# When the FFN output weights' sums are begun, and which queue carries their copies: a fused decoder layer on Trainium2

## The chip, the cores and the metric

The kernel runs on one core of one Trainium2 chip. The metric is device time in microseconds (us) of one execution, inputs in the device's memory at its start and the output written at its end. The engines of the core are called as in the profile: PE (TensorE, matmuls; PEld its weight loads), DVE (VectorE), ACT (ScalarE), POOL (GpSimd), SP (SyncE). SPq, ACTq and POOLq stand for the instruction streams in which these engines issue DMAs. Each engine works through its stream in order.

## The reference

One layer of a decoder trunk on a sequence of 512 tokens of width 1024, in fp32:

```python
h = rms_norm(x, norm_mix)
q_a, k_a, v_a, u_b, gate_b, gate_c, g_a, g_b = split(h @ w_in)        # 1024 -> 5120
o_a = stick_breaking_attention(q_a, k_a, v_a)                         # 8 heads of 64, causal
y_b = gate_b * causal_depthwise_conv(gate_c * u_b, conv_w)            # 3 taps, 512 channels
merged = sigmoid(g_a) * (o_a @ w_branch_a) + sigmoid(g_b) * (y_b @ w_branch_b)
x = x + merged @ w_mix_out
x = x + memory_cross_attention(rms_norm(x, norm_mem_q), rms_norm(mem, norm_mem_kv),
                               w_mem_q, w_mem_kv, w_mem_o)            # 4 heads of 256, 256 memory tokens
gate, up = split(rms_norm(x, norm_ffn) @ w_ffn_in)                    # 1024 -> 2 x 2816
x = x + (silu(gate) * up) @ w_ffn_out                                 # 2816 -> 1024
return rms_norm(x, norm_final)
```

## The kernel before, in words

Activations lie with channels on the 128 partitions and the 512 tokens along the free axis, so that a width of 1024 is eight tiles. An fp32 product is made of three matmuls in a shorter format: each operand is split into a high part (a cast on ACT) and a low part (a subtraction on DVE), and high by high, high by low and low by high are added up (`mm3`, L161 to L163). `load_w` brings a weight tile of 512 KB (tile `wr`, L148, issued on SP), casts it to `wh` (L156, ACT) and subtracts for `wl` (L157, DVE); four buffers of each are in turn. So a late cast or split makes a `wr` buffer free late, and the load that is to use it is issued late.

The stages, with their places in the profiled execution: the input projection and the attention (to about 160 us), the merge with its gates and branch projections (a loop over eight output tiles m), the mixer's output projection (`residual` on `w_mix_out`, eight tiles; tile `r`; to about 344), the memory's keys (`km`, eight tiles, 344 to 367), half of the values (`vm`), the query forms and the rest of the values (367 to 400), the four memory heads (scores `sc`, maximum `mx`, bound `nb`, exps `pr`, transposes `pt`, output `om`; to about 464), the memory's output projection (`residual` again, on `w_mem_o`), the FFN's first weights (`ws`, `wg`, `a`), and the FFN's output weights in the last stage.

Some products use sums of weight quarters, in the manner of Strassen's method. Two kinds of sums are made ahead of their use.

- The sums of the FFN's output weights, 11 sets j = 0 to 10 (`out_sums`). A set is two copies from DRAM to DRAM (768 and 256 KB, L569, on SP) and then three adds by POOL's DMAs (512, 256 and 256 KB, L572), which add to the tile in DRAM where it lies (`sums`). A step waits for the landing of the step before. The last stage reads them, from about 700 us on.
- The sums of the memory's query weights, one per head: a load of 1 MB (`pq`, L642), three additions on DVE, a store of 1 MB to DRAM (`qsums`, L652), in the merge and the mixer's output projection.

What sets the order of the sums is a counter of ticks. `job(at, steps, lag)` puts the steps of a set at ticks `at`, `at + lag` and so on; `tick(last)` issues what stands at the present tick behind the instruction `last` in program order. The steps of the sums do not wait for that instruction on the chip, only for their data and for their place in their engine's stream. Ticks come 17 times in the attention (0 to 16), 8 times in the merge (17 to 24), at every second tile of the mixer's output projection (25 to 28), twice in the keys' loop (29, 30), once after the first values (31), and once per memory head (32 to 35). `SUMS_AT` is the list of the first ticks, and `SPARSE` says how many sets take two ticks per step in place of one.

Between the mixer's output projection and the memory heads, the factor r1 of the second norm is needed with tokens on partitions. It goes through DRAM (`turned_row`): a row `vrow` of 2 KB is stored (L226, `row`) and loaded back as `vr` (L228), both on SP; ACT then makes `ry` of it (L125, L126) and DVE `ra` and `r` (L129 to L133). The same helper, on POOL's stream, serves a later norm (`r0b`, `row`, `rt`).

`pair_forms` (L810 to L812) loads the query weights and their sums and splits them into `wf`; `q_product` (L834 to L855) multiplies them (`qz`, `qv`) and copies the results out (`qs`, `qb`).

Of the kernel before, what the change touches and what calls it, by code (L numbers as in the profile page):

```python
# [34 lines left out]
FIRST = 4  # L35
LIGHT = 3
BEHIND = 6
SUMS_AT = (0, 2, 4, 20, 22, 24, 25, 26, 27, 28, 30)
SPARSE = 3

O_Q, O_K, O_V, O_U, O_GB, O_GC, O_A, O_B = 0, 512, 1024, 1536, 2048, 2560, 3072, 4096

# [2 lines left out]
def hybrid_layer(ctx: ExitStack, tc: tile.TileContext, xT_d, memT_d, mem_d, cols_d, wv_d, win_d,  # L45
                 wbr_d, wmix_d, wmq_d, wmk_d, wmv_d, wmo_d, wfi_d, wfo_d, gfin_d, out):
    nc = tc.nc
# [16 lines left out]
    def nm(s):  # L64
        count[0] += 1
        return f"{s}{count[0]}"

    def unit(s, cols=512):
        return upool.tile([P, cols], F32R, tag="u", name=nm(s), padded_shape=[P, 512])

    def tmp(s, cols=512):
        return tpool.tile([P, cols], F32, tag="t", name=nm(s), padded_shape=[P, 512])

    def f(ap):
        return ap.bitcast(F32)

    def mmtile(s, pool=None, tag="mm"):
        return (pool or pmm).tile([P, 512], F32, tag=tag, name=nm(s))
# [28 lines left out]
    def after(i, earlier):  # L107
        for e in earlier:
            tc.add_manual_dep(i.ins, e.ins.name, mybir.DependencyInfo(
                mybir.DependencyClass.NoSync, mybir.DependencyReason.DATA), reason="order")  # L110
# [33 lines left out]
    def load_w(src, cols=P):  # L144

        k = D // cols
        raw = wpool.tile([P, D], F32, tag="wr", name=nm("wr"))
        i = nc.sync.dma_start(raw, src)  # L148
        loads.append(i)
        if count[1] < FIRST:  # L150
            count[1] += 1
            chained(i)
        hi = wpool.tile([P, k, cols], F32R, tag="wh", name=nm("wh"))
        lo = wpool.tile([P, k, cols], F32R, tag="wl", name=nm("wl"))
        h2, l2 = (t.rearrange("p k c -> p (k c)") for t in (hi, lo))
        after(nc.scalar.copy(h2, raw), lead[-1:])  # L156
        lows.append(nc.vector.tensor_tensor(out=l2, in0=raw, in1=f(h2), op=ALU.subtract))  # L157
        return hi, lo
# [8 lines left out]
    def gemm(ps, w, act, k0=0):  # L167

        n = len(act)
        for k in range(n):  # L170
            if k == n // 2 and midway:
                midway.pop()()
            mm3(ps, (w[0][:, k0 + k, :], w[1][:, k0 + k, :]), act[k], k == 0, k == n - 1)
# [277 lines left out]
    def scores(p, kt):  # L451
        c0, n = span(kt)
        keys = slice(kt * P, (kt + 1) * P)
        zs[p, kt] = []
        for hs in heads_of(kt):
            bank = ztile("z")
            zs[p, kt].append(bank)
            for i, h in enumerate(hs):
                for part in range(2):
                    nc.tensor.matmul(bank[:, i * n:(i + 1) * n], ks[p][h][:, keys],  # L460
                                     qs[p][h][part][:, c0:], start=i + part == 0, stop=part == 1,
                                     skip_group_check=True)
        for hs, bank in zip(heads_of(kt), zs[p, kt]):
            w = len(hs) * n
            z = bank[:, :w]
            e = tmp("e")[:, :w]
            nc.scalar.activation(e, z, AF.Abs)
            nc.scalar.activation(e, e, AF.Exp, scale=-1.0)
            nc.scalar.activation(e, e, AF.Ln, bias=1.0)
            nc.vector.scalar_tensor_tensor(out=e, in0=z, scalar=0.0, in1=e, op0=ALU.max,  # L470
                                           op1=ALU.add)
            causal(by_head(e, n))
            urgent.append(lambda *last, e=e, hs=hs: fails(p, kt, hs, e, n, last))
# [86 lines left out]
    def quarters(w):  # L560
        return w.rearrange("p (s c) -> p s c", s=4)

    def in_dram(tag):
        return dpool.tile([P, 4, 512], F32, tag=tag, name=nm(tag))

    sums = [in_dram(f"sums{j}") for j in range(NJ)]

    def copied(to, of):
        return lambda *last: after(nc.sync.dma_start(to, of), last)  # L569

    def added(to, of):
        return lambda *last: after(nc.gpsimd.dma_start(to, of, accum_op=ALU.add), last)  # L572

    def out_sums(j):
        t, w = sums[j], quarters(wfo_d[j])
        return ([copied(t[:, 1:4, :], w[:, 1:4, :]), copied(t[:, 0:1, :], w[:, 3:4, :])],
                [added(t[:, 0:4:3, :], w[:, 0:2, :])], [added(t[:, 1:2, :], t[:, 0:1, :])],
                [added(t[:, 2:3, :], t[:, 1:2, :])])

# [2 lines left out]
    def job(at, steps, lag=1):  # L582
        for n, some in enumerate(steps):
            jobs.setdefault(at + n * lag, []).extend(some)

    def tick(*last):
        for some in jobs.pop(started[0], ()):
            some(*last)
        started[0] += 1
# [14 lines left out]
    settle_behind()  # L604
    qsums = [in_dram(f"qsums{h}") for h in range(MH)]
    for j, n in enumerate(SUMS_AT):
        job(n, out_sums(j), 2 if j < SPARSE else 1)

    for i in range(len(steps) + 1):
        tick(*exps[-1:])  # L610
# [10 lines left out]
        if i + 1 < len(steps):  # L621
            to = lambda: scores(*steps[i + 1])
# [15 lines left out]
    mg, mgs, qraws = [], [], {}  # L638

    def form_load(h, last):  # L640
        qraws[h] = prepool.tile([P, 4, 512], F32, tag="pq", name=nm("pq"))
        after(nc.sync.dma_start(qraws[h], quarters(wmq_d[h])), last)  # L642

    def form_sums(h, last, *steps):

# [3 lines left out]
                                          op=ALU.add), last)  # L649

    def form_store(h):
        nc.sync.dma_start(qsums[h], qraws.pop(h))  # L652

    def mem_split(k2, last):
        mk = xpool.tile([P, 2, MEM], F32, tag="x", name=nm("mk"))
# [15 lines left out]
    for m in range(KD):  # L671
        sig = []
        for j in range(2):
            if (m, j) not in gates:
                gate(m, j)
            t = gates.pop((m, j))
# [5 lines left out]
        w = load_w(wbr_d[m])  # L682
# [74 lines left out]
    def residual(w_dram, act, old, gain, formed):  # L757


        xs, xf = [], []  # L760
        acc = tmp("acc")
        for m in range(KD):
            w = load_w(w_dram[m])
            ps = mmtile("r")
            gemm(ps, w, act)
            if old is None:
                xm = xpool.tile([P, S], F32, tag="x", name=nm("x"))
                after(nc.sync.dma_start(xm, xT_d[m * P:(m + 1) * P, :]), sigmoids[m // 2 - 4])
            else:
                xm = old[m]  # L770
            nc.vector.tensor_tensor(out=xm, in0=ps, in1=xm, op=ALU.add)
            xs.append(xm)
            if old is None and m % 2:
                tick(lows[-1])
                if qraws:
                    form_store(MH - 1)
            raw = f(unit("xr"))
            nc.scalar.activation(raw, xm, AF.Copy, scale=gain[:, m:m + 1])
            if m % 2:
                xf.append(formed(even, raw))  # L780
            else:
                even = raw
            if m == 0:
                nc.scalar.activation(acc, xm, AF.Square)
            else:
                sq = tmp("sq")
                nc.scalar.activation(sq, xm, AF.Square)
                nc.vector.tensor_tensor(out=acc, in0=acc, in1=sq, op=ALU.add)
        return xs, xf, (lambda: squares_mean(acc, TT))

    x1, x1f, mean1 = residual(wmix_d, merged, None, g_q, flat_forms)
    mean1 = mean1()
    stick.close()
# [82 lines left out]
    for m in range(KD):  # L876
        w = load_w(wmk_d[m])
# [8 lines left out]
        t = tmp("km", MEM)  # L886
# [52 lines left out]
    for h in range(MH):  # L939
        q = qgot[h]  # L940
        scs = []
        for t2 in range(2):
            ps = ztile("sc")
            scs.append(ps)
            for i in range(2):
                t = 2 * t2 + i
# [5 lines left out]
        for t2 in range(2):  # L952
# [14 lines left out]
            for i in range(2):  # L967
                t = 2 * t2 + i
# [25 lines left out]
        for j in range(2):  # L994
# [3 lines left out]
            for m in range(MT):  # L998
                w = vm[m][c // 512]
                mm3(ps, (w[0][:, sl], w[1][:, sl]), ptr[m], m == 0, m == MT - 1)  # L1000
            om.append(split(ps, "om"))

    lead.append(qacts[-3])
    x2T, x2f, mean2 = residual(wmo_d, om, x1, g_ffn, forms_of)


# [141 lines left out]
    m = NF - 1  # L1148
# [96 lines left out]
    def one_cast(j):  # L1245
        if j % 2 == 0:
            n = min(2, NJ - j)
            raw = ows["q3"] = wpool.tile([P, 2, 512], F32, tag="wr", name=nm("wr"))
            nc.sync.dma_start(raw[:, :n, :], wfo_d[j:j + n, :, 0:512].rearrange("j p c -> p j c"))
        raw = ows["q3"][:, j % 2, :]  # L1250
        pool, tag = (fpool, "wg") if j in (BEHIND, BEHIND + 2) else (wpool, ("wh", "wl")[j % 2])
        w = pool.tile([P, 2, 512], F32R, tag=tag, name=nm("wq"))
        nc.scalar.copy(w[:, 0, :], raw)
        ows[5, j] = w[:, 0, :], w[:, 1, :]
        return raw, *ows[5, j]
# [75 lines left out]
    n = uses.index((NF - 2, 5))  # L1331
# [23 lines left out]
    with tc.manual_schedule(engines={mybir.EngineType.PE, mybir.EngineType.Activation,  # L1355
# [58 lines left out]
        for j in range(2, NJ - 2):  # L1414
# [6 lines left out]
            if NJ - 2 - LIGHT <= j + 1 < NJ - 2 + 1:  # L1421
                n = j + 1 - (NJ - 2 - LIGHT)
                if n < LIGHT:
                    t34_of(n, halves(acts[n][1])[0])
        last = NJ - 2, NJ - 1
# [93 lines left out]
        w = one_cast(NJ - 1)  # L1519
# [184 lines left out]
```

## Time and profile before

| | |
|---|---|
| time, median of 3 runs | 835.94 us (835.62 to 836.13) |
| profiled execution, its own time | 837.15 us |
| its span, first to last instruction | 835.4 us |
| mean granted TensorE clock | 0.998 |
| PE busy | 826.5 us (99% of the span) |
| ACT busy | 481.8 us (58%) |
| issues of the sums: copies on SP, adds on POOL | 22, 33 |
| DMA bytes by SP's queues and by POOL's | 130.96 MB, 23.21 MB |

Rows of the profile give the engine, the line, the operation, the tile written and the tiles read; in the views by time the first number is the start in us from the span's start, the second the length, and a bracket at the end tells how long the engine had been idle before and what ended that. "DMA share" is the mean busy share of the 16 DMA engines. A DMA's "us to landing" counts from its issue.

### The profile page before, as it was taken

The page shows a single profiled execution, that of the slowest core. Times are in us where ns is not written, and L with a number is a line of the kernel's source. Part 1 is how long each engine was busy: PE and PEld are TensorE (multiplying, and loading weights), DVE is VectorE, ACT ScalarE, POOL GpSimd, SP SyncE. Part 2 cuts the span into 40 slices and gives each one's busy share as a digit, 9 for nine tenths or more (in the row PEclk, how much of TensorE's full clock was granted, in tenths as well). Part 3 has the DMA queues.
Part 4 walks back from the last instruction along what each step waited for, and adds up shares of the span by engine and source line. Part 5 has one row for each costly group of instructions (what it writes and reads, how often), then busy time and mean ns, then how long its engine had stood idle before and what let it go on. Part 6 is the DMA issues. An engine that isn't in the chain of part 4 may idle for free.

```text
span 835.4 us, 12382 instructions
## 1 busy us (share of the span) xinstructions
PE 826.5 (99%) x4518; PEld 718.7 (86%) x4518; DVE 689.6 (83%) x1146; ACT 481.8 (58%) x836; POOL 105.9 (13%) x131
## 2 busy tenths in 40 slices
PE   9999999999999999999999999999999999999996
PEld 7888888888888888888999789999999999888885
DVE  7879899995665557865677689999999999999886
ACT  7567777674332345645665556645555555576664
POOL 0022331120010011210000131111111110000301
PEclk9999999999999999999999999999999999999999
DMA  8667965224588999898445626677777773565552
GB/s 303 202 189 179 222 141 121 82 81 171 216 225 291 253 312 294 194 218 279 125 136 189 167 50 170 165 179 189 207 179 196 181 181 97 166 217 198 178 187 100
DMA packets 58926, 155.24 MB, mean 186 GB/s; under 512 B 6545, under 2 KB 7825, under 8 KB 57842
## 3 DMA queue, kind: packets, MB, share of 16 engines
q1 hardware_dynamic: 46226, 130.96, 46.6%
q0 software_dynamic: 12352, 23.21, 18.5%
q8 instruction: 35, 0.57, 0.3%
q10 hardware_dynamic: 288, 0.28, 0.1%
q14 instruction: 25, 0.20, 0.1%
HBM read 144.08 MB, written 29.37 MB: 208 GB/s over the span
## 4 chain that ended last, share of the span: by engine, by line
PE 95%; DMA 2%; DVE 1%; ACT 1%; issue 0%; DVEq 0%; SPq 0%; ACTq 0%
PE z L1078 13%; PE p L1389 12%; PE pr L161 8%; PE pr L162 8%; PE pr L163 8%; PE y L1073 5%; PE r L161 3%; PE r L163 3%; PE r L162 3%; PE v L288 3%; PE y L1081 2%; PE v L1073 2%; PE qz L834 2%; PE br L162 2%; PE br L161 2%; PE br L163 2%
## 5 line engine op out<-in xcount | busy, mean ns | idle before, releaser
L156 ACT CAST wh<-wr 128x1024 fp32r<-128x1024 f32 x76 | 79.7, 1051 | 113.0 <-issue 45.1
L161 PE MATMUL pr<-xgh,wh 128*128 128x512 f32 x288 | 112.7, 391 | 0.0
L162 PE MATMUL pr<-xgl,wh 128*128 128x512 f32 x288 | 112.4, 390 | 0.0
L163 PE MATMUL pr<-xgh,wl 128*128 128x512 f32 x288 | 112.3, 390 | 0.0
L157 DVE TENSOR_TENSOR wl<-wr,wh 128x1024 fp32r<-128x1024 f32 x76 | 93.6, 1232 | 9.8 <-ACT wh L156 9.5
L163 PEld LDWEIGHTS pr<-xgh,wl 128*128 128x128 f32 x288 | 54.1, 188 | 11.5
L161 PEld LDWEIGHTS pr<-xgh,wh 128*128 128x128 f32 x288 | 54.1, 188 | 10.6
L162 PEld LDWEIGHTS pr<-xgl,wh 128*128 128x128 f32 x288 | 54.1, 188 | 10.5
L1026 POOL DMA_DIRECT2D ws<-in_w_ffn_in_dram x22 | 26.6, 1207 | 237.5 <-PE pt L987 57.1
L1078 PE MATMUL z<-xd,wf 128*128 128x256 f32 x360 | 47.5, 282 | 0.0
L1110 ACT COPY sa<-z 128x256 f32<-128x256 f32 x44 | 16.5, 374 | 52.1 <-PE z L1078 52.0
L1078 PEld LDWEIGHTS z<-xd,wf 128*128 128x128 f32 x360 | 44.9, 190 | 0.1
L1170 DVE TENSOR_TENSOR wf<-wg,wf 128x1024 fp32r<-128x1024 f32 (+1 forms) x44 | 43.1, 979 | 1.5
L1170 DVE TENSOR_TENSOR wl<-wr,wh 128x1024 fp32r<-128x1024 f32 x33 | 41.1, 1247 | 3.6 <-ACT wh L1237 3.6
L368 DVE TENSOR_TENSOR g<-pr,r0b 128x512 f32<-128x512 f32 x16 | 11.0, 689 | 34.2 <-PE pr L163 34.2
L1237 ACT CAST wh<-wr 128x1024 fp32r<-128x1024 f32 x33 | 34.5, 1049 | 6.9 <-PE xt L1474 2.5
L1078 PE MATMUL z<-xf,wf 128*128 128x256 f32 x264 | 35.4, 283 | 0.0
L1078 PE MATMUL z<-xc,wf 128*128 128x256 f32 x264 | 35.1, 282 | 0.0
L1078 PEld LDWEIGHTS z<-xf,wf 128*128 128x128 f32 x264 | 33.4, 192 | 0.1
L1078 PEld LDWEIGHTS z<-xc,wf 128*128 128x128 f32 x264 | 33.0, 190 | 0.0
L572 POOL DMA_DIRECT2D sums<-sums x22 | 18.5, 851 | 94.7 <-DMA sums<-in_w_ffn_out_dram 47.4
L572 POOL DMA_DIRECT2D sums<-in_w_ffn_out_dram x11 | 15.7, 1469 | 98.7 <-DMA sums<-in_w_ffn_out_dram 98.2
(377 smaller groups left out, 2313.8 us busy)
## 6 DMA issues: line engine op xcount, KB each, us to landing
wr<-in_w_in_dram SPq DMA_DIRECT2D x36, 512.0 KB, 4.1
ws<-in_w_ffn_in_dram SPq DMA_DIRECT2D x22, 512.0 KB, 4.6
wg<-in_w_ffn_in_dram SPq DMA_DIRECT2D x22, 512.0 KB, 4.5
ws<-in_w_ffn_in_dram POOLq DMA_DIRECT2D x22, 512.0 KB, 5.8
wr<-sums SPq DMA_DIRECT2D x22, 512.0 KB, 4.4
sums<-in_w_ffn_out_dram SPq DMA_DIRECT2D x11, 768.0 KB, 8.1
wr<-in_w_ffn_out_dram SPq DMA_DIRECT2D x16, 512.0 KB, 4.5
sums<-in_w_ffn_out_dram POOLq DMA_DIRECT2D x11, 512.0 KB, 10.2
```

The lines of the kernel that those rows point to most:

```text
L156: after(nc.scalar.copy(h2, raw), lead[-1:])
L157: lows.append(nc.vector.tensor_tensor(out=l2, in0=raw, in1=f(h2), op=ALU.subtract))
L161: nc.tensor.matmul(ps, a[0], b[0], start=start, stop=False, **kw)
L162: nc.tensor.matmul(ps, a[0], b[1], start=False, stop=False, **kw)
L163: nc.tensor.matmul(ps, a[1], b[0], start=False, stop=stop, **kw)
L572: return lambda *last: after(nc.gpsimd.dma_start(to, of, accum_op=ALU.add), last)
L1026: nc.gpsimd.dma_start(s13, a[:, 0:4:3, :], accum_op=ALU.add)
L1073: nc.tensor.matmul(ps, hi, both[0], start=i < 3 and k == 0, stop=False, skip_group_check=True)
L1078: nc.tensor.matmul(ps[:, :HS], a, b, start=i < 3 and k == 0 and j == 0, stop=k == KP - 1 and j == 2, skip_group_check=True)
L1170: nc.vector.tensor_tensor(out=lo, in0=src, in1=f(hi), op=ALU.subtract)
L1237: nc.scalar.copy(hi, raw)
L1389: nc.tensor.matmul(res[i][s2], a[:, ts], b, start=j == 0 and n == 0, stop=n == 2 and j == (BEHIND - 1 if (i, s2) == (5, 1) else NJ - 1))
```

## The change

The list of first ticks is new: sets 0 to 3 are in the attention, three ticks apart, and the last three begin at ticks 32, 34 and 36. `SPARSE` is 4. The copies of sets 4 to 10 are issued on ACT; so are the loads and stores of the query weights' sums. `residual` now ticks in the memory's output projection too (ticks 36 to 39). Line numbers after L577 are higher by one in the changed kernel.

```diff
-SUMS_AT = (0, 2, 4, 20, 22, 24, 25, 26, 27, 28, 30)
-SPARSE = 3
+SUMS_AT = (0, 3, 6, 9, 19, 22, 26, 30, 32, 34, 36)
+SPARSE = 4
...
-    def copied(to, of):
-        return lambda *last: after(nc.sync.dma_start(to, of), last)
+    def copied(queue, to, of):
+        return lambda *last: after(queue.dma_start(to, of), last)
...
-    def out_sums(j):
+    def out_sums(j, queue):
         t, w = sums[j], quarters(wfo_d[j])
-        return ([copied(t[:, 1:4, :], w[:, 1:4, :]), copied(t[:, 0:1, :], w[:, 3:4, :])],
+        return ([copied(queue, t[:, 1:4, :], w[:, 1:4, :]),
+                 copied(queue, t[:, 0:1, :], w[:, 3:4, :])],
                 [added(t[:, 0:4:3, :], w[:, 0:2, :])], [added(t[:, 1:2, :], t[:, 0:1, :])],
...
-        job(n, out_sums(j), 2 if j < SPARSE else 1)
+        job(n, out_sums(j, nc.sync if j < SPARSE else nc.scalar), 2 if j < SPARSE else 1)
...
-        after(nc.sync.dma_start(qraws[h], quarters(wmq_d[h])), last)
+        after(nc.scalar.dma_start(qraws[h], quarters(wmq_d[h])), last)
...
-        nc.sync.dma_start(qsums[h], qraws.pop(h))
+        nc.scalar.dma_start(qsums[h], qraws.pop(h))
...
-            if old is None and m % 2:
+            if m % 2:
                 tick(lows[-1])
```

In the rows of the order below, the number behind a name tells one buffer of it from another; `sums_374` to `sums_384` are the sets 0 to 10, in both kernels.

SP's stream before, where the loads for the memory's keys begin: the copies of sets 8 and 9 stand between them.

```order
L148 DMA wr_3347<-in_w_mem_k_dram 128x1024
L569 DMA sums_382<-in_w_ffn_out_dram 128x1536
L569 DMA sums_382<-in_w_ffn_out_dram 128x512
L148 DMA wr_3378<-in_w_mem_k_dram 128x1024
L148 DMA wr_3425<-in_w_mem_k_dram 128x1024
L569 DMA sums_383<-in_w_ffn_out_dram 128x1536
L569 DMA sums_383<-in_w_ffn_out_dram 128x512
L148 DMA wr_3456<-in_w_mem_k_dram 128x1024
```

After the change the loads there stand alone:

```order
L148 DMA wr_3268<-in_w_mix_out_dram 128x1024
L148 DMA wr_3337<-in_w_mem_k_dram 128x1024
L148 DMA wr_3368<-in_w_mem_k_dram 128x1024
L148 DMA wr_3415<-in_w_mem_k_dram 128x1024
L148 DMA wr_3446<-in_w_mem_k_dram 128x1024
```

The copies of sets 8 and 9 have left this place, and no copy of a set stands in SP's stream behind the attention any more.

ACT's stream before, at the end of the keys' loop, where the query forms begin:

```order
L156 CAST wh_3670<-wr_3668 128x1024
L887 COPY km_3602<-km_3585 128x256
L894 CAST kmh_3575<-km_3602 128x256
L811 CAST wf_3697<-wr_3696 128x1024
L811 CAST wf_3703<-wr_3702 128x1024
```

And after:

```order
L156 CAST wh_3656<-wr_3654 128x1024
L888 COPY km_3590<-km_3573 128x256
L569 DMA sums_381<-in_w_ffn_out_dram 128x1536
L895 CAST kmh_3563<-km_3590 128x256
L569 DMA sums_381<-in_w_ffn_out_dram 128x512
L812 CAST wf_3682<-wr_3681 128x1024
L812 CAST wf_3688<-wr_3687 128x1024
```

The two copies of set 7 stand there now; before, set 10's copies were issued from SP's stream at that tick.

DVE's stream before, in the last memory head, between the last weight split ahead of the scores and the exps' bounds:

```order
L157 TENSOR_TENSOR wl_4778<-wr_4775,wh_4777 128x1024
L955 TENSOR_REDUCE mx_4576<-sc_4550 128x2
L955 TENSOR_REDUCE mx_4588<-sc_4563 128x2
L958 SCALAR_TENSOR_TENSOR nb_4578<-mx_4576,r1s 128x2
L958 SCALAR_TENSOR_TENSOR nb_4590<-mx_4588,r1s 128x2
```

And after:

```order
L956 TENSOR_REDUCE mx_4567<-sc_4541 128x2
L157 TENSOR_TENSOR wl_4774<-wr_4771,wh_4773 128x1024
L959 SCALAR_TENSOR_TENSOR nb_4569<-mx_4567,r1s 128x2
L956 TENSOR_REDUCE mx_4579<-sc_4554 128x2
L959 SCALAR_TENSOR_TENSOR nb_4581<-mx_4579,r1s 128x2
```

The split of the fourth weight of the memory's output projection has moved from ahead of the first maximum to behind it. On PE, seven matmuls of that projection (`r`) stand ahead of the first scores of this head, where one stood; the eighth stands among the scores, where three stood.

## The prediction

> **What bounds the kernel now.** I read the page first, for who is busy.
>
> ```profile
> span 835.4 us, 12382 instructions
> PE 826.5 (99%) x4518; PEld 718.7 (86%) x4518; DVE 689.6 (83%) x1146; ACT 481.8 (58%) x836; POOL 105.9 (13%) x131
> ```
>
> TensorE (PE) is busy for 826.5 of 835.4 us. A change that touches no matmul can win only PE's 8.9 us of idle time and whatever is hidden inside "busy". So the second view is PE's own waits, and the third its busy time by stretches of the span. The columns of that one are length, PE, weight load, DVE, ACT and POOL busy time, the granted clock, the DMA engines' share and GB/s.
>
> ```profile
> PE warm L248 <- DVE neg L92: 1.4, 1, 1.4
> PE qz L834 <- ACT qs L845: 0.7, 1, 0.7
> PE vm L161 <- DVE km L888: 0.4, 1, 0.4
> ...
> 354.00:366.00 12.00, 12.00 (x69) 10.51 (x68) 5.87 (x11) 4.61 (x11) 1.66 (x2) 1.00 1.05 240
> 374.00:386.00 12.00, 11.29 (x74) 10.17 (x73) 8.20 (x11) 6.72 (x10) 1.17 (x1) 1.00 0.94 296
> 440.00:460.00 20.00, 20.00 (x137) 17.93 (x135) 13.69 (x28) 11.27 (x25) 0.79 (x1) 1.00 0.61 206
> 518.00:528.00 10.00, 10.00 (x75) 9.48 (x74) 9.83 (x19) 6.39 (x9) 1.69 (x4) 1.00 0.66 164
> 820.00:836.00 16.00, 9.01 (x54) 7.83 (x52) 9.57 (x26) 7.99 (x22) 2.70 (x2) 0.89 0.35 131
> ```
>
> The last stretch leaves 7.0 us that this change does not touch, and the first wait, 1.4 us at the start, is as far from it. What remains are two waits in the middle: vm and qz, both in 366 to 386. A third fence, of PE's rows in order of time, shows how much they really cost.
>
> ```profile
> 366.96 0.39 PE L161 MATMUL vm<-wh,mg 128*128 128x512 f32 x1
> 368.52 0.50 PE L161 MATMUL vm<-wh,mg 128*128 128x512 f32 x1 [0.42 <-DVE km L888]
> 369.08 0.39 PE L163 MATMUL vm<-wh,mg 128*128 128x512 f32 x1
> 378.63 0.39 PE L163 MATMUL vm<-wh,mg 128*128 128x512 f32 x1
> 384.59 0.28 PE L834 MATMUL qv<-xfh,wf 128*128 128x256 f32 x1
> 385.58 0.39 PE L834 MATMUL qz<-xfh,wf 128*128 128x256 f32 x1 [0.71 <-ACT qs L845]
> ```
>
> From 369.08 to 378.63 there are 42 steps of 512 columns, 0.227 us each, with no wait. From 366.96 to 369.08 there are five, which at that pace take 1.14 us and here take 2.12: stall 1 costs 0.98. A 256-column step takes about half of that, 0.12; the one from 384.59 to 385.58 takes 0.99: stall 2 costs 0.87. Together 1.85 us is what is to be had, just above the 1.67 us (0.2% of 835.94) that a measurement of this kernel can tell from no change.
>
> The chain of waits names what both hang on, and ScalarE's and GpSimd's rows show it standing.
>
> ```profile
> 354.73 5.07 DMA row<-vrow
> 359.81 5.61 DMA vr<-row
> 366.10 1.22 DVE wl L157
> ...
> 374.86 7.54 DMA wr<-in_w_mem_q_dram
> ...
> 365.45 0.30 ACT L125 ACTIVATE ry<-vr,eps_t 128x4 f32<-128x4 f32 x1 [4.30 <-DMA vr<-row]
> 384.21 1.05 ACT L156 CAST wh<-wr 128x1024 fp32r<-128x1024 f32 x1 [1.11 <-DVE qa L843]
> ...
> 356.10 0.85 POOL L572 DMA_DIRECT2D sums<-sums  x1 [3.56 <-DMA sums<-sums]
> 362.56 0.81 POOL L572 DMA_DIRECT2D sums<-sums  x1 [5.61 <-DMA sums<-in_w_ffn_out_dram]
> ```
>
> The factor r1 of the second norm goes through DRAM: 2 KB out, 2 KB back, 10.7 us, in a stretch where the DMA share is 1.05 and adds of the sums are on their way (two wait for one another's landings on POOL here). ACT works in order and stands 4.30 us on it; DVE stands behind ACT, and behind DVE the split (wl) of the first memory value weights, which vm needs: stall 1. The same lateness passes through the weight slots that such splits free to the query load of 374.86, its cast, and the weight cast of 384.21 that stands ahead of the copy qs: stall 2.
>
> **The change part by part.** *Times of the sums.* Of the eleven sets, j=3 to 10 had their copies at ticks 20 to 30; now j=3 is in the attention, j=4, 5, 6 are at 19, 22, 26, j=7 at 30 and j=8 to 10 at 32, 34, 36. The order puts the first copy of j=6 right behind the weight cast that now runs at 306.12 (last row below). From there the copies, the big add and the two small ones take 8.1 + 10.2 + 6.7 + 6.7 us, to 339 (an estimate). The copies of j=7 stand behind km's last copy to SBUF, near 368, as PE leaves km at 366.96. Between them no set is on the way, and the round trip meets only weight loads. Its price is bounded above by its own 10.7 us and below by the same pair of hops in 518 to 528, where the share is 0.66:
>
> ```profile
> sums<-in_w_ffn_out_dram SPq DMA_DIRECT2D x11, 768.0 KB, 8.1
> sums<-in_w_ffn_out_dram POOLq DMA_DIRECT2D x11, 512.0 KB, 10.2
> sums<-sums POOLq DMA_DIRECT2D x22, 256.0 KB, 6.7
> ...
> row<-r0b POOLq DMA_DIRECT2D x1, 2.0 KB, 4.5
> rt<-row POOLq DMA_DIRECT2D x1, 2.0 KB, 2.9
> ...
> 306.12 1.05 ACT L156 CAST wh<-wr 128x1024 fp32r<-128x1024 f32 x1 [3.18 <-PE r L162]
> ```
>
> That is 7.4 us. I take it, since weight loads alone are what ran there too: r1's row lands at 362.1 in place of 365.4, 3.3 us earlier. Stall 1 needs 1.0 us of that, and the copy qs must come 1.9 us earlier, because PE is there 1.0 us sooner. Both fit, with 1.4 us to spare: minus 1.85 us. At the other end of the bound nothing is won. By the Trainium skill ("DMA: Bandwidth & Descriptors", the part on the anatomy of one DMA), a DMA has about 2.0 us of fixed cost, which would make two hops 4.0 us and the gain no larger, since the stalls are gone before; the rows with 2.9 and 4.5 us say that it is more here.
>
> *Copies and query sums on ScalarE's queue.* 14 copies, four loads (pq) and four stores (qsums), 22 issues in all, leave SP's stream and enter ACT's.
>
> ```profile
> 373.13 1.14 SPq L569 DMA_DIRECT2D sums<-in_w_ffn_out_dram  x2
> ...
> 0.79 0.40 ACTq L236 DMA_DIRECT2D gcol<-in_columns_dram  x1
> ...
> 437.25 0.56 ACT L969 ACTIVATE pr<-sc,nb,r1s 128x256 f32<-128x256 f32 x1 [1.61 <-DVE nb L958]
> ```
>
> An issue costs 0.40 us on ACT's one row and 0.57 on SP's pairs: 8.8 to 12.5 us of an engine that is busy 58%. The residual lets ACT idle for 3.18 us ahead of a cast (306.12), which a pair of 0.8 to 1.14 fits into; a store that waits for DVE's sum holds only casts that wait for PE anyway. In the heads the two copies of a set stand before and after pr, where 1.61 us are free. I cost it at nothing; if that cover went, each copy would put 0.40 to 0.57 us on pr and on the transposes behind it. On SP the loads behind 373.13 are issued 1.14 us sooner, which adds to the slack of stall 2. The sum has nothing in it for faster landings. By the Trainium skill (same page, "Issuing engines are not separate DMA queues") transfers of all issuing engines run on the same 16 DMA engines, so that this move saves issue time only; no run here shows it, since the load of 7.54 us right behind two copies may be late by the engines' load or by its queue's order.
>
> *Fourth set in the attention.* PE has no idle time there. The additions cost POOL 0.85 us each beside its mask selects, and the sets start three ticks apart in place of two. Bounds: 0, and 0.85 if one select on the path stands behind one add. I take 0, because PE's waits name nothing in the attention now.
>
> *Late sets, head 3.* The order moves matmuls of the output projection (r) ahead of the last scores, and a weight split between mx and nb.
>
> ```profile
> 455.57 0.56 ACT L969 ACTIVATE pr<-sc,nb,r1s 128x256 f32<-128x256 f32 x1 [3.85 <-DVE nb L958]
> 457.69 0.60 PE L987 MATMUL pt<-ident,pr 128*128 128x128 f32 x4
> ```
>
> Before, pr starts at 455.57 and PE comes to pt at 457.69, without a wait. Now four more r steps of 0.23 us stand ahead of the scores' end and one fewer behind it: PE comes to pt 0.7 us later. The split of 1.22 us (the wl row) between mx and nb, less the half of the scores that is no longer waited for, makes pr late by about 0.7 too (estimates from these rows). Between 0 and 0.7 us are at stake; I take 0, because the two move together.
>
> *Late sets, FFN's start.* POOL's loads of the FFN weights now have adds between them; such a load may come late:
>
> ```profile
> 471.90 1.21 POOL L1026 DMA_DIRECT2D ws<-in_w_ffn_in_dram  x1 [11.45 <-DVE c L713]
> 490.19 0.62 ACT L1059 CAST wf<-ws 128x512 fp32r<-128x512 f32 x1 [2.65 <-PE r L162]
> ```
>
> From its issue to its use there are 18.3 us. If it stood behind an add that lands in 10.2, 8 us would be left for it. Nothing.
>
> Sum: minus 0.98 and minus 0.87, the rest 0: minus 1.85. Against the profiled execution's own 837.15 us (the span and 1.75 around it) this gives 835.30; the median of the runs is 1.21 below the profiled execution, so 834.1.
>
> **The rivals.** *A, half of it.* The two stalls are not equally safe. The copies of j=7 still fall beside the query loads, as those of j=10 did, and now on a queue of their own. If the load of 374.86 keeps its landing at 382.4, stall 2 stays and grows by the 1.0 us that PE is early: a gain between 0 and 0.98, 834.9 to 835.9. For it speaks the 0.94 share in 374 to 386; against it the 3.3 us.
>
> *B, no change.* The 1.05 share of 354 to 366 may come from the weight loads themselves, which now run sooner: the round trip keeps its 10.7 us, 835.9. Against it: the software queue of the adds is what goes.
>
> *C, slower: a late weight in head 3.* By the order, two sets are now copied between 436 and 460, beside the exps (pr) of heads 2 and 3, where the share is 0.61 and mem_o's weights come in.
>
> ```profile
> wr<-in_w_mem_o_dram SPq DMA_DIRECT2D x8, 512.0 KB, 3.8
> DMA to landing us min/median/max: 6.0/8.1/15.5
> ...
> 440.56 0.69 DVE L812 TENSOR_TENSOR wf<-wr,wf 128x512 fp32r<-128x512 f32 x1
> ```
>
> The second row is that of the copies. The fourth mem_o weight is issued at about 441.3, when the query split of 440.56 has freed its slot, and its cast (1.05) and split (1.22) now stand ahead of pr and nb. With 3.8 us it is there at 445; with the copies' median at 449.4, still early. For pr at 455.57 as now, cast and split must start by 453.3 (455.57 less 1.05 and 1.22): from a landing of 12.0 us on, PE waits one for one. At the copies' largest, 15.5, it is 3.5 us, and the time 834.1 + 3.5 = 837.6. The gain is eaten at 13.9 us. By the Trainium skill (same page, on queues, rings and completion order) each DMA engine takes turns between queues with work, packet by packet; a load on SP's queue would then share its engines with ACT's copies rather than go ahead of them, about twice 3.8 us, which this place bears.
>
> **How the numbers follow.** Forecast 0.48 (833.6 to 834.6), A 0.23, B 0.14, C or the attention's 0.85 with the stalls kept 0.15. The forecast falls below 834.27 (faster by over 0.2%) in some three quarters of its cases: 0.37. The last case, counted from 837.6 with what A may add, gives its 0.15 to slower (above 837.61). The rest, 0.48, lies within 0.2%. The range runs from 833.6, the forecast less the 0.5 us by which the three runs differ, to 837.2, most of C's stall: 0.06 and 0.13 are left out.
>
> **What would show it.** Right: no wait of PE in 360 to 390; the row vr<-row landing at 361 to 363; no idle of 4 us ahead of ry; no sums add of POOL between 340 and 368; the query load by 379. Stall 2 alone still there is A; a round trip above 9.5 us is B; a PE wait on pt or om in 450 to 463 is C, and one in the attention the 0.85. The prediction is wrong too if a merge cast waits behind a store on ACT's queue.

## The result and the profile after

The changed kernel takes 846.17 us (median of 4 runs, 844.53 to 849.32) against 836.04 us before (835.62 to 836.39): a ratio of 1.0126, interval 1.0096 to 1.0156. It is slower by 10.1 us, where 834.1 was forecast and 837.2 was the top of the range. Two executions far from all others (1672.23 us of the kernel before, 2128.87 us of run 9) are in none of the ratios below. The profiled execution took 849.32 us, with a span of 847.6, which is 12.2 us more than the span before.

The page of the kernel after, with the rows that answer to those of before (the last is TensorE's clock in 40 slices):

```profile
span 847.6 us, 12382 instructions
PE 829.8 (98%) x4518; PEld 720.5 (85%) x4518; DVE 693.5 (82%) x1146; ACT 482.9 (57%) x836; POOL 104.9 (12%) x131
PEclk9999999799999999999999999999999999999999
```

PE has the same 4518 instructions, 3.3 us more busy time and, by span less busy, 17.8 us of idle time in place of 8.9. The one 7 in the clock, in the eighth slice (148 to 170 us), points to the attention. PE's own waits, after:

```profile
PE z L460 <- issue: 8.3, 1, 8.3
PE warm L248 <- DVE neg L92: 1.4, 1, 1.4
PE z L1079 <- DVE xf L720: 0.9, 1, 0.9
PE z L506 <- DVE l L432: 0.6, 1, 0.6
```

Both stalls of the middle (vm 0.4, qz 0.7) are gone. In their place stands one wait of 8.3 us in the attention, on a product of queries and keys (z, L460), and two small ones. PE's busy time by stretches shows the same, first before:

```profile
146.00:155.00 9.00, 9.00 (x45) 7.62 (x44) 8.97 (x18) 5.37 (x12) 1.88 (x3) 1.00 0.37 117
155.00:160.00 5.00, 5.00 (x24) 4.17 (x23) 3.78 (x7) 4.27 (x7) 1.44 (x3) 1.00 0.13 26
```

and then after:

```profile
146.00:155.00 9.00, 0.72 (x5) 0.33 (x3) 4.12 (x8) 0.04 (x1) 1.76 (x3) 0.71 0.76 166
155.00:160.00 5.00, 5.00 (x15) 4.04 (x16) 1.43 (x3) 1.63 (x4) 1.23 (x2) 0.50 0.47 188
```

In the nine microseconds PE does 0.72 us of work, and in the next five it is "busy" all the time but starts 15 matmuls in place of 24, at a granted clock of 0.50. The DMA share is two to four times that of before. The chain of waits of the kernel after (start, length, what) gives both parts their size:

```profile
146.48 8.28 issue
154.75 1.08 PE z L460 x4
155.83 0.53 PE pr L161
156.37 0.43 PE pr L162
...
159.35 0.43 PE pr L163
```

Ten matmuls of 512 columns, to 160.00, run at about 0.43 us in place of 0.23: 2.1 us. The matmul behind the four small z starts 0.88 us after them, by PE's rows in order of time, and 0.39 before. So the place costs 8.3 + 2.1 + 0.5 = 10.9 us (11.0 by the start times of the same matmuls in both profiles, below).

"Issue" as a releaser names no one. What z reads are tiles `qk`: `qk_parts` (L361) moves the queries and keys of a head pair from SBUF to SBUF, in nine moves of 128 KB (six for queries, three for keys) issued on SP. SP's rows of before, in the window of the last head pair (start, length with the queue's waits in it):

```profile
117.92 15.18 SPq L361 DMA_DIRECT2D qk<-qk  x6
133.19 0.54 SPq L148 DMA_DIRECT2D wr<-in_w_in_dram  x1
133.84 7.19 SPq L361 DMA_DIRECT2D qk<-qk  x3
```

and after:

```profile
121.21 5.86 SPq L361 DMA_DIRECT2D qk<-qk  x5
127.11 0.59 SPq L569 DMA_DIRECT2D sums<-in_w_ffn_out_dram  x1
135.99 0.46 SPq L361 DMA_DIRECT2D qk<-qk  x1
136.50 0.89 SPq L569 DMA_DIRECT2D sums<-in_w_ffn_out_dram  x1
137.44 0.64 SPq L148 DMA_DIRECT2D wr<-in_w_in_dram  x1
138.19 10.47 SPq L361 DMA_DIRECT2D qk<-qk  x3
```

The fourth set's copies stand among the moves. SP stands before some of the moves until earlier ones have landed: the last was issued at 148.19, when another had landed at 148.18 (that is the 10.47 us for three). How long each took is in the DMA rows of the trace. The last key move alone, and all moves of this pair (us to landing), before:

```profile
qk<-qk SPq DMA_DIRECT2D x1, 128.0 KB, 2.2
DMA to landing us min/median/max: 2.2/6.6/12.0
```

and after:

```profile
qk<-qk SPq DMA_DIRECT2D x1, 128.0 KB, 6.5
DMA to landing us min/median/max: 4.6/9.6/15.6
```

Before, the last move was issued at 140.57 and landed at 142.77. After, it was issued at 148.19 and landed at 154.66, and PE started z at 154.75. PE's and POOL's rows, PE's of before first, then PE's and POOL's of after:

```profile
145.21 0.56 PE L460 MATMUL z<-qk,qk 128*128 128x128 f32 x4
...
154.75 1.08 PE L460 MATMUL z<-qk,qk 128*128 128x128 f32 x4 [8.28 <-issue]
...
124.35 0.89 POOL L572 DMA_DIRECT2D sums<-sums  x1
125.92 0.85 POOL L572 DMA_DIRECT2D sums<-sums  x1 [0.19 <-issue]
147.13 1.19 POOL L572 DMA_DIRECT2D sums<-in_w_ffn_out_dram  x1 [1.91 <-DMA sums<-in_w_ffn_out_dram]
```

Before, z came at 145.21 without a wait, on data that had landed at 142.77: **the slack was 2.4 us**, and no view of waits shows it. After, two adds of 256 KB (14.8 and 16.1 us to landing, on the way until 139 and 142), the fourth set's copies of 768 and 256 KB, and from 147.13 its add of 512 KB were on the way beside the moves. Before, in the same stretch, there was one add (issued at 124.83, landed at 137.06).

### The profile page after: what moved, and what is told of

Its sections match the earlier page's. It is cut to its first block, busy times and chain, and to the rows that moved or that the text cites. A ratio compares the mean times of both kernels' runs of the same rounds, so it can differ in the third digit from the quotient of the medians.

```text
span 847.6 us, 12382 instructions
## 1 busy us (share of the span) xinstructions
PE 829.8 (98%) x4518; PEld 720.5 (85%) x4518; DVE 693.5 (82%) x1146; ACT 482.9 (57%) x836; POOL 104.9 (12%) x131
## 4 chain that ended last, share of the span: by engine, by line
PE 94%; DVE 3%; issue 1%; DMA 1%; ACT 1%; DVEq 0%
PE z L1079 12%; PE p L1390 12%; PE pr L161 7%; PE pr L162 7%; PE pr L163 7%; PE y L1074 5%; PE r L163 3%; PE r L162 3%; PE r L161 3%; PE qz L835 3%; PE v L288 3%; PE y L1082 2%; PE v L1074 2%; PE qv L835 2%; PE km L882 2%; PE br L163 2%
## 5 line engine op out<-in xcount | busy, mean ns | idle before, releaser
L161 PEld LDWEIGHTS pr<-xgh,wh 128*128 128x128 f32 x288 | 54.7, 190 | 10.7
L162 PEld LDWEIGHTS pr<-xgl,wh 128*128 128x128 f32 x288 | 54.7, 190 | 10.7
L572 POOL DMA_DIRECT2D sums<-in_w_ffn_out_dram x11 | 13.0, 1183 | 189.8 <-DMA sums<-in_w_ffn_out_dram 189.4
```

The lines of the kernel that those rows point to most:

```text
L161: nc.tensor.matmul(ps, a[0], b[0], start=start, stop=False, **kw)
L162: nc.tensor.matmul(ps, a[0], b[1], start=False, stop=False, **kw)
```

## The experiments

Two parts of the change meet in the attention: the first sets' wider spacing (ticks 0, 3, 6 for 0, 2, 4), and the fourth set at tick 9. The first four kernels take them apart, and take the rest of the change by itself.

**1. Wide spacing, no fourth set in the attention** (set 3 goes to tick 17, one tick per step, its copies on ACT).

```diff
-SUMS_AT = (0, 3, 6, 9, 19, 22, 26, 30, 32, 34, 36)
-SPARSE = 4
+SUMS_AT = (0, 3, 6, 17, 19, 22, 26, 30, 32, 34, 36)
+SPARSE = 3
```

> The changed kernel with its fourth set (j=3) moved out of the attention, to ticks 17 to 20, its copies on ScalarE's queue; sets 0 to 2 stay three ticks apart. Theory (the copies of the fourth set stand in SP's stream among the last moves of queries and keys, and those come late for the scores): PE's wait on the scores' matmul (8.3 us) and the ten matmuls at 427 ns behind it are gone, the middle's 1.85 us stay won, the 1.4 us at the FFN's start and some 0.4 in the heads stay lost: 835.7 to 836.4, ratio 0.998 to 1.002. Rival 1 (the wider spacing of sets 0 to 2 puts the adds of set 2 beside those moves): a wait of several us stays, 840 or more.

Measured: 837.32 us, ratio 1.0015 (1.0005 to 1.0025). Nearly all of the loss is gone with the one set, and no matmul runs at half clock. But z has no slack left:

```profile
146.80 0.63 PE L460 MATMUL z<-qk,qk 128*128 128x128 f32 x4 [0.51 <-DMA qk<-qk]
```

Here the releaser is named: the move. The spacing alone uses up the 2.4 us, and the kernel stays just slower than before, although it keeps the gain in the middle (no wait on vm or qz is left in its profile).

**2. The fourth set's copies on ACT's queue**, so that they are out of SP's stream of moves.

```diff
-        job(n, out_sums(j, nc.sync if j < SPARSE else nc.scalar), 2 if j < SPARSE else 1)
+        job(n, out_sums(j, nc.sync if j < 3 else nc.scalar), 2 if j < SPARSE else 1)
```

> The changed kernel with the copies of the fourth set on ScalarE's queue in place of SP's, at the same ticks. Theory in its narrow form (place in SP's stream): the moves are issued on time, PE's wait falls below 2 us, 836 to 838.5. Rival 2 (bytes: the same copies slow the moves in whichever queue they are): wait of 4 to 9 us as in the changed kernel, 842 to 848.

Measured: 844.25 us, ratio 1.0096 (1.0079 to 1.0113). The wait is still there:

```profile
PE z L460 <- issue: 6.6, 1, 6.6
```

So the place of the copies in SP's stream is worth some 1.7 us of the wait between these two profiles; the rest is not their place. What of it are the copies' bytes and what the adds behind them, this run does not tell; run 6 does. By the Trainium skill ("DMA: Bandwidth & Descriptors", "Issuing engines are not separate DMA queues"), DMAs of all issuing engines run on the same 16 DMA engines and interleave there. This run agrees with that.

**3. The fourth set alone, put into the kernel before.**

```diff
-SUMS_AT = (0, 2, 4, 20, 22, 24, 25, 26, 27, 28, 30)
-SPARSE = 3
+SUMS_AT = (0, 2, 4, 9, 22, 24, 25, 26, 27, 28, 30)
+SPARSE = 4
```

> The kernel before with one edit: set j=3 in the attention at ticks 9, 11, 13, 15 (copies on SP) in place of tick 20. Theory: this alone brings the wait on the scores, 4 to 9 us, and the slow matmuls: 841 to 847, ratio 1.006 to 1.014. Rival 1 (spacing of sets 0 to 2, which stays as before here): no wait, 835.5 to 837.

Measured: 836.31 us, ratio 1.0002 (0.9992 to 1.0012), and z runs unwaited:

```profile
145.39 0.56 PE L460 MATMUL z<-qk,qk 128*128 128x128 f32 x4
```

The theory that the fourth set does it alone falls. It needs the spacing, as the spacing needs it. But "unwaited" is again not "free": the last key move was issued at 142.85, where it was 140.57 before, and by the best landing of such a move, 2.2 us, that leaves at most 0.3 us of slack (an estimate; the trace has no landing for this move).

**4. The rest of the change without both**: first sets as before, none more in the attention, the others spread so that the middle has none.

```diff
-SUMS_AT = (0, 3, 6, 9, 19, 22, 26, 30, 32, 34, 36)
-SPARSE = 4
+SUMS_AT = (0, 2, 4, 17, 19, 21, 23, 25, 30, 32, 34)
+SPARSE = 3
```

> The changed kernel with the first ticks 0, 2, 4, 17, 19, 21, 23, 25, 30, 32, 34: three sets in the attention as before, none on the way between about 340 and 368, the last one two ticks earlier. Theory: no wait in the attention, both stalls of the middle gone, and the adds before the FFN's weight loads on POOL's queue done in time, so the 1.4 us at the FFN's start shrink to 0.5 or less: 834.0 to 834.8, ratio 0.9975 to 0.9985. Rival 3 (the issues on ScalarE's queue or more traffic in the merge cost on their own): 835.5 or more.

Measured: 835.37 us, ratio 0.9988 (0.9979 to 0.9997). No wait of PE is left in the middle, and the time falls, but by 1.0 us (0.3 to 1.8), less than the 1.85 that the two stalls had in the one profile.

**5. The change with narrow spacing**: the fourth set stays at tick 9.

```diff
-SUMS_AT = (0, 3, 6, 9, 19, 22, 26, 30, 32, 34, 36)
+SUMS_AT = (0, 2, 4, 9, 19, 22, 26, 30, 32, 34, 36)
```

> The changed kernel with the first four ticks 0, 2, 4, 9 in place of 0, 3, 6, 9: the fourth set stays in the attention, the first three keep the spacing of the kernel before. Theory, as the runs so far leave it (the fourth set's copies and the adds of the three sets, made late by the spacing, are in flight together beside the moves of queries and keys; either alone costs at most 0.7 us): no wait on the scores over 0.5 us, no slow matmuls, 835.2 to 836.4, ratio 0.999 to 1.000. Rival 4 (the fourth set costs in this kernel whatever the spacing, since its other copies are on ScalarE's queue): a wait of several us, 840 or more.

Measured: 835.95 us, ratio 0.9994 (0.9984 to 1.0003); z at 144.91 without a wait, 2.3 us behind the landing of the last move (142.60). Runs 3 and 5 have the same four first ticks, so how much slack is left differs by some 2 us between two profiles. Two numbers in the list are the whole loss. With runs 1, 3 and 4 the table is complete (PE's wait on z, us):

| | no fourth set | fourth set at tick 9 |
|---|---|---|
| sets 0 to 2 at 0, 2, 4 | none (before, run 4) | none (runs 3 and 5) |
| sets 0 to 2 at 0, 3, 6 | 0.5 (run 1) | 8.3 (after), 6.6 (run 2) |

**6. The change with the fourth set's adds held back to tick 17**, its copies left at tick 9.

```diff
-        job(n, out_sums(j, nc.sync if j < SPARSE else nc.scalar), 2 if j < SPARSE else 1)
+        steps_j = out_sums(j, nc.sync if j < SPARSE else nc.scalar)
+        if j == 3:
+            job(n, steps_j[:1])
+            job(17, steps_j[1:])
+        else:
+            job(n, steps_j, 2 if j < SPARSE else 1)
```

> The changed kernel with the three adds of the fourth set at ticks 17 to 19, its copies at tick 9 as they were. Theory: the last key move, which landed in 6.5 us beside the set's first add and in 2.2 without one, lands in 2 to 3 us; the wait on the scores falls by some 4 us to 3 to 5, the slow matmuls stay: 840 to 843. Rival 5 (the copies' bytes alone delay the last move): wait and time as in the changed kernel, 844.5 to 849.

Measured: 841.48 us, ratio 1.006 (1.0042 to 1.0078). The last move landed in 2.2 us again, and the wait fell from 8.3 to 2.1:

```profile
148.27 0.64 PE L460 MATMUL z<-qk,qk 128*128 128x128 f32 x4 [2.14 <-issue]
```

So the last move's delay is the first add of the fourth set. It comes when the add is ahead of the move: issued 1.06 us ahead of it in the kernel after and 1.07 in run 2, where the move landed in 6.5 and 6.3 us. In run 5 the move had landed (142.60) before the add was issued (143.68), and in run 7, below, the add was only 0.52 us ahead and the move landed in 2.3. The 2.1 us that stay lie in the moves ahead of the last one, beside which the two copies and the late adds of sets 1 and 2 still run; run 1, with the late adds alone, has 0.5 of it, so by subtraction between two profiles the copies have the rest.

**7. The change with only the third set late** (ticks 0, 2, 6, 9).

```diff
-SUMS_AT = (0, 3, 6, 9, 19, 22, 26, 30, 32, 34, 36)
+SUMS_AT = (0, 2, 6, 9, 19, 22, 26, 30, 32, 34, 36)
```

> The changed kernel with the first four ticks 0, 2, 6, 9: only the third set (j=2) is late, as in the change, the second at tick 2 as before. Theory (the third set's adds, the big one issued near 117 in place of 98, are what meets the fourth set's copies beside the moves): a wait on the scores of 4 to 9 us, 841 to 847. Rival 7 (the second set's last add, near 109, is needed too): a wait under 2 us, 835.5 to 838.

Measured: 838.89 us, ratio 1.005 (1.0028 to 1.0073), in two groups: five runs at 837.4 to 838.9 and four at 841.0 to 845.3, with the profiled one at 841.0 and a wait of 1.8 us on z. It lies between the two expectations: the third set's lateness makes a part of the loss, and the rest needs the second set's as well. How much each makes in a given execution is not settled, since the times of one kernel jump by more than the parts. In the profiled one the add just missed the last move (0.52 us ahead, 2.3 to landing); whether the two executions at 845 us are ones in which it did not is not shown, since no profile is of one of them.

**8. The kernel before once more**, no edit, to see whether its stalls are the same in another execution.

> The kernel before, profiled once more. The profile of the prediction was 1.2 us above the median of its runs. If the two stalls of the middle (0.98 and 0.87 us there) are as long in every execution, they are again 1.8 to 1.9 us together whatever the time; if they vary with the landing of the norm's row, the time less the stalls is 835.3 again and the stalls are shorter when the time is near 836.

Measured: 835.38 us (one execution). Its waits of PE, and ACT at the factor r1:

```profile
PE warm L248 <- DVE neg L92: 1.4, 1, 1.4
PE qz L834 <- ACT qs L845: 0.4, 1, 0.4
...
364.11 0.30 ACT L125 ACTIVATE ry<-vr,eps_t 128x4 f32<-128x4 f32 x1 [1.08 <-DMA vr<-row]
```

The wait on vm is not there at all, the one on qz is 0.4 in place of 0.7, and ACT stands 1.08 us in place of 4.30. The round trip took 9.7 us in place of 10.7. PE's matmuls start 0.35 us earlier than in the first profile up to the middle (343.05 and 342.70), and 1.72 earlier behind it (400.01 and 398.29): 1.4 of the 1.8 us between these two executions of one kernel are the stalls. The profile that the prediction was worked out from had caught the middle in a worse execution than this one.

**9 and 10. Run 4 with everything on SP's queue** (copies, query sums' loads and stores), the same kernel measured twice.

```diff
-SUMS_AT = (0, 3, 6, 9, 19, 22, 26, 30, 32, 34, 36)
-SPARSE = 4
+SUMS_AT = (0, 2, 4, 17, 19, 21, 23, 25, 30, 32, 34)
+SPARSE = 3
...
-        job(n, out_sums(j, nc.sync if j < SPARSE else nc.scalar), 2 if j < SPARSE else 1)
+        job(n, out_sums(j, nc.sync), 2 if j < SPARSE else 1)
...
-        after(nc.scalar.dma_start(qraws[h], quarters(wmq_d[h])), last)
+        after(nc.sync.dma_start(qraws[h], quarters(wmq_d[h])), last)
...
-        nc.scalar.dma_start(qsums[h], qraws.pop(h))
+        nc.sync.dma_start(qsums[h], qraws.pop(h))
```

> The kernel with the quiet middle (three sets in the attention, first ticks 0, 2, 4, 17, 19, 21, 23, 25, 30, 32, 34) with all copies and the query sums' transfers on SP's queue, as before the change. Theory: the queue is worth nothing, 835.1 to 835.7, ratio 0.9985 to 0.9995 to the kernel before. Rival 6 (SP's loads wait behind the copies in its stream): a wait of PE on a late weight in the merge or the heads, 836.5 or more.

> The kernel with the quiet middle and all transfers on SP's queue once more, for a profile and a second measurement. Theory: no wait of PE in the attention, the middle or the heads over 0.4 us, 834.5 to 835.2, ratio 0.998 to 0.999. Rival 6 (the first measurement was luck, SP's loads wait behind the copies): 835.8 or more, with a wait on a late weight.

Measured: 834.87 us, ratio 0.9983 (0.9973 to 0.9994), and 835.25 us, ratio 0.9989 (0.9981 to 0.9998). The waits are read from the second's profile, where the wait at the start is the only one that PE has. Against run 4 (0.9988) the queue makes no difference that these intervals can tell. This version beats both kernels, by 0.9 to 1.4 us on before.

## Why the prediction was wrong

**The step that failed** is the "Fourth set in the attention": bounds 0 and 0.85 us, "I take 0, because PE's waits name nothing in the attention now". It measured about 11 us. Three things were wrong in it. It counted the adds' issues on POOL and not the transfers: what the adds and copies do to the moves of queries and keys, which stand in SP's stream at this very place, was not asked. It read "no wait" as "no cost", where the last move's landing (142.77) and z (145.21) would have given a margin of 2.4 us, one move's own spread: in this stretch moves landed in 2.2 to 12.0 us. And it did not ask what spacing and set do together: against the kernel before, the set alone costs 0.2 us (run 3, not clear of noise), the spacing with the rest of the change 1.2 (run 1; some 2 above run 4, which has neither), and both together ten.

**The two small waits.** POOL's issue does hold a mask select, as the 0.85 said: in the kernel after, two selects behind an add take 2.00 us, where the same two took 0.54 before. PE's wait of 0.6 us on `l` (L506) follows at 114.3. But the select is not what makes it: run 7 has the same wait (0.56) and no add ahead of its selects. The first row is of the kernel after, the second of run 7.

```profile
109.87 2.00 POOL L417 TENSOR_SCALAR_AFFINE_SELECT a<-a 128x128 f32<-128x128 f32 x2
...
109.58 0.54 POOL L417 TENSOR_SCALAR_AFFINE_SELECT a<-a 128x128 f32<-128x128 f32 x2
```

What goes with the wait in every profile is an earlier one, of ACT, on a load of the memory's tokens (`mk`). Before, after, and run 7:

```profile
98.08 0.63 ACT L549 ACTIVATE mk<-mk 128x512 f32<-128x512 f32 x1 [1.44 <-DMA mk<-in_mem_dram]
99.19 0.63 ACT L549 ACTIVATE mk<-mk 128x512 f32<-128x512 f32 x1 [3.13 <-DMA mk<-in_mem_dram]
99.21 0.63 ACT L549 ACTIVATE mk<-mk 128x512 f32<-128x512 f32 x1 [3.04 <-DMA mk<-in_mem_dram]
```

ACT stands 3.0 to 3.6 us on this load in the five profiles that have the wait (after, runs 1, 2, 6 and 7), and at most 1.7 in the six others. The casts of `l` stand behind it on ACT, and DVE's subtraction for `l` comes at 100.36 in place of 99.24 and has not caught up when PE wants `l`. The place costs 1.2 us, twice what the view of waits shows: PE's matmuls start 0.08 us earlier than before ahead of it (112.83 and 112.75) and 1.09 later behind it (114.11 and 115.20). So here too a load came late beside the sums, and not a select; what made this load late no run isolates.

At the FFN's start, "Nothing" came out as a wait of 0.9 us. POOL's stream now holds adds between the loads of the FFN's weights, and the load ahead of its first additions is issued at 500.10, where it was 485.96 before: 14.1 us later, while PE reaches the FFN only 10.6 us later (511.68 and 501.10). POOL's addition then falls beside DVE's:

```profile
500.10 1.24 POOL L1027 DMA_DIRECT2D ws<-in_w_ffn_in_dram  x1 [8.38 <-DMA ws<-in_w_ffn_in_dram]
502.75 1.63 POOL L1043 TENSOR_TENSOR a<-wg 128x512 f32<-128x512 f32 x1
...
503.15 1.50 DVE L712 TENSOR_TENSOR c<-xr 128x256 f32<-128x256 f32 x1
...
517.46 0.50 PE L1079 MATMUL z<-xf,wf 128*128 128x256 f32 x2 [0.87 <-DVE xf L720]
```

In run 1, POOL's addition was over before, the same c took 0.41 us and PE did not wait; in run 7, c took 1.51 us beside such an addition, and PE waited 0.87 again. DVE is then 1.1 us late in a chain without slack. That the overlap is the cause is read from rows; no run isolates it. Runs 1, 2, 5 and 6 have the same late sets and no such wait, run 7 has it: it hangs on where the two additions happen to fall.

**The stalls of the middle.** The mechanism was right: without sets in the middle, ry has no idle time ahead of it, and stalls 1 and 2 vanish, in the kernel after and in runs 4 and 10.

```profile
366.80 0.30 SPq L226 DMA_DIRECT2D row<-vrow  x1
368.00 0.52 SPq L228 DMA_DIRECT2D vr<-row  x1
371.16 0.30 ACT L125 ACTIVATE ry<-vr,eps_t 128x4 f32<-128x4 f32 x1
```

The round trip, landed at 371.01, took 4.2 us, at a DMA share of 0.63 from 366 to 372. The estimate of 7.4, which the prediction took for a lower bound, was too high: its pair of hops went by POOL's stream, and these two go by SP's. The price of two hops by the Trainium skill, 4.0 us ("DMA: Bandwidth & Descriptors", the part on the anatomy of one DMA, which gives it for DMAs that GpSimd issues), was the nearer one. The gain was not larger for it, as the prediction said. Between the two profiles it was 2.0 us, close to the 1.85. But against the median it was smaller: 0.9 to 1.4 by the ratios of runs 4, 9 and 10, and run 8 shows one reason: the stalls are not the same in every execution. The prediction took 1.85 off the profiled execution and then 1.21 for that execution's distance from the median. By run 8 a part of that distance is the stalls themselves, and that part was taken off twice.

**ACT's issues at nothing** held: runs 4, 9 and 10 differ in the queue alone and not in time. **Head 3 at 0** nearly held, and rival C did not occur: PE has no wait on pt or om after, and its matmuls lose 0.3 us from 403.88 to 470.05. Rivals A and B did not either. The slower side came from the place that the prediction had only as "the attention's 0.85", inside the 0.15 that it shared with C.

**The sum as it is**, by the start times of the same matmuls in the two profiles: PE is 1.1 us later behind `l` (114.11 and 115.20), 12.1 behind z (150.02 and 162.09), 10.0 behind the stalls of the middle (400.01 and 410.03), 10.6 at the end of the heads (470.05 and 480.63) and 12.2 behind the FFN's start (506.55 and 518.73). So z costs 11.0 us, `l` 1.2, the FFN's start 1.6 and the query forms and heads 0.6, and the middle gives back 2.0: to 0.2 us the whole of the 12.17 between the two executions (849.32 and 837.15). The three waits show 9.8 us of these losses; the rest is hidden in "busy", as it was for the two stalls.

## What to carry to other kernels

Before traffic is added to a stretch where the bound engine has no waits, measure for each DMA that feeds it the time from its landing to its use, and set that against the spread of its landings; a view of waits shows only what is late already. Test edits of one list together as well as apart, since two that each fit into the same 2.4 us of slack need not fit together. And take a stall from more than one execution before pricing its removal, or price it against that execution and not against the median as well.

## What the runs showed of the hardware

Half clock came after much shorter waits than 8.3 us. In run 6 PE stood 2.1 us, in run 7 1.8 us, and then seven matmuls of 512 columns ran at 0.43 us each, some 3 us at half clock (the granted clock from 148 to 152 us is 0.66 in run 6 and 0.57 in run 7). Run 6, PE's rows, from 1.4 us behind its wait:

```profile
149.63 0.63 PE L161 MATMUL pr<-xgh,wh 128*128 128x512 f32 x1
150.06 0.63 PE L162 MATMUL pr<-xgl,wh 128*128 128x512 f32 x1
150.48 0.63 PE L163 MATMUL pr<-xgh,wl 128*128 128x512 f32 x1
```

Run 1's wait of 0.5 us brought none. So in these two profiles a wait of about 2 us cost 1.4 us more behind it (7 x 0.2). By the Trainium skill ("TensorE: Matmul & The Clock Gate", Part 1) the clock falls after an idle window of some 3.4 us that runs free of the kernel; these two waits were shorter than that, and here the measurement decides.

A move of 128 KB inside SBUF landed in 2.2 us at best. Issued 1.06 us behind an add of 512 KB the same move took 6.5, with the DMA share at 1.04 from 149 to 155 us, though only 215 GB/s were moved; issued 0.52 us behind one (run 7) it took 2.3. Two weight loads were issued right behind the move in all these cases.
